# A state-space layer's carried products in halves of 64 rows: states kept in the scan's rows, two PSUM banks by the group's parity, and the third batch's W asked for later

## The chip, the cores and the metric

The kernel runs on one core of a Trainium2 chip. The metric is the device time of one execution in microseconds (us), the median of several. A profile of one execution gives the start and the length of every instruction on TensorE (PE, with its weight loads as PEld), VectorE (DVE), ScalarE (ACT), GpSimd (POOL) and the DMA queues, of which SyncE's (SP) carries nearly all loads.

## The reference

A trunk of two residual layers over 256 tokens of 2048 features: RMSNorm, a convolution module, RMSNorm, an MLP with squared ReLU; then the same with the state-space module in place of the convolution. Only the state-space module is touched:

```
u = h.reshape(bsz, L, 128, 16)                    # 128 groups of 16 channels
bu = einsum("blgc,gpc->blgp", u, bb)              # complex, 64 states a group
_, _, s_re, s_im = associative_scan(combine, (a, bu), axis=1)
y = einsum("blgp,gcp->blgc", s_re, c_re) - einsum("blgp,gcp->blgc", s_im, c_im)
y = gelu(y.reshape(bsz, L, 2048) + d_skip * h)
z = y @ w_glu;  val, gate = split(z, 2);  return val * sigmoid(gate)
```

All of it is in float32.

## The kernel before

The large products stream weights of 1 MB a step through SP; ACT rounds each half step to a high part (`hi`, L118), DVE forms the low part (`lo`, L125), and PE multiplies high by high, high by low and low by high (L222 to L224 in the layer at hand). A step has two halves of 12 such products. Three raw buffers are in turn, and a load is asked for when the low part of the step three before it is done.

The state-space layer sits between the first MLP and the second. The tokens are cut into 32 blocks of 8 (`CH`), and the scan runs over blocks. The groups are worked in four batches B of 32, each as 8 values g by 4 quarters q (the quarter picks 32 columns of the TensorE array and 32 partitions of PSUM). For a batch:

- `ssm_front` multiplies the inputs by table W (into the states), `ssm_turn` transposes, `ssm_scan` turns the complex scan into two real ones on DVE (`S`), and `ssm_forth` turns the result back (two products of 128x1024 into `t`).
- `ssm_states` forms the states `SS` from `t`. In the scan's layout the 128 rows are 64 states of two neighbouring groups: rows 0 to 63 belong to the group of even g, rows 64 to 127 to that of odd g. Before the change, `SS` has the real part in rows 0 to 63 and the imaginary part in rows 64 to 127, for each group; so each parity takes two DVE instructions over 64 rows, four in all, which move halves of the rows across.
- `ssm_local` multiplies the inputs by table M (what a block gives to itself); `ssm_carry` adds the states by table V (what is carried in) to the same PSUM banks `A`: 32 products, each over 128 rows, of 32 columns and 128 outputs. The two banks hold g 0 to 3 and 4 to 7. A float32 product shows in the trace as two matmul records with a weight load each. `ssm_carry` ends with GELU on ACT, and `ssm_out` transposes `y` into the features for the large product.

V is made during the first MLP as background work: 16 times `vstage` (three DVE products into the buffer `bv`, then one DMA on POOL's queue into `Vd` in DRAM), with `kstage` and `mstage` behind it, which make M.

`begin` writes the order for batches 0 and 1 by hand, before the first product with `w_glu`; batches 2 and 3, and what is left of batch 1, are put between half steps by the table `todo` (`carry(1)` in step 1, `carry(2)` in step 7, `carry(3)` in step 11). W, M, V, `xJ`, `S` and `yT` share the pool `blk` of six buffers. Which buffer a tile gets, and so what its load waits for, follows from the order in which the tiles are asked for. The loads of SP keep the order in which they are written.

Of the kernel before, what the change touches and what calls it, by code (L numbers as in the profile page):

```python
# [9 lines left out]
F32 = mybir.dt.float32  # L10
F32R = mybir.dt.float32r
I32 = mybir.dt.int32
AF = mybir.ActivationFunctionType
ALU = mybir.AluOpType
# [4 lines left out]
P = 128  # L19
# [8 lines left out]
G, ST, GC = 128, 64, 16  # L28
CH = 8
VW = PAD + T + 2  # L30
NQ = 4
# [5 lines left out]
class Trunk:  # L37
# [823 lines left out]
    def ssm_prep(self):  # L861
        nc, a, bg = self.nc, self.a, self.bg
# [2 lines left out]
        self.Wd = self.dram.tile([P, G, P], F32, name="Wd")  # L865
        self.Kd = self.dram.tile([G, GC, 15 * GC], F32, name="Kd")
        self.Md = self.dram.tile([P, G, P], F32, name="Md")
        self.Vd = self.dram.tile([P, G, P], F32, name="Vd")
        self.Bd = self.dram.tile([G, 2, ST, GC], F32, name="Bd")
        self.Rd = self.dram.tile([P, NQ, 1024], F32, name="Rd")  # L870
        self.xs = self.dram.tile([T, D], F32, name="xs")
        dma = nc.gpsimd.dma_start
# [221 lines left out]
        def vstage(k):  # L1094
            vs = s["bv"][:, 1, 0:1152].rearrange("p (g d c) -> p g d c", d=9, c=GC)
            g = slice(8 * k, 8 * k + 8)
            c = [s["c12"][:, i, g, :].unsqueeze(2).broadcast_to([P, 8, 8, GC]) for i in range(2)]
            p = [s[x][:, g, :].unsqueeze(3).broadcast_to([P, 8, 8, GC]) for x in ("pr", "pi")]
            t = self.t4([P, 8, 8, GC], name="vt")
            v = vs[:, :, 1:9, :]  # L1100
            self.tt(v, c[0], p[0], ALU.mult)
            self.tt(t, c[1], p[1], ALU.mult)
            self.tt(v, v, t, ALU.add)
            nc.scalar.activation(vs[:, :, 0, :], s["c12"][:, 0, g, :], AF.Copy)
            dma(out=self.Vd[:, g, :], in_=v.rearrange("p g d c -> p g (d c)"))

        def kstage(k):
            vs = s["bv"][:, 1, 0:1152].rearrange("p (g x) -> p g x", x=9 * GC)
# [17 lines left out]
        for k in range(16):  # L1126
            add(12, lambda k=k: vstage(k))
            add(4 if k < 4 else 3, lambda k=k: kstage(k))
            if k >= 4:
                for d in range(2 * (k % 4), 2 * (k % 4) + 2):  # L1130
                    add(0.5, lambda B=k // 4 - 1, d=d: mstage(B, d))
# [51 lines left out]
    def table(self, kind, B):  # L1183

        if kind == "R":
            t = self.t4([P, 2, 16, 32], name="R") if B != 2 else self.S[:, 1]
            self.fetch(t.rearrange("p i g j -> p (i g j)"), self.Rd[:, B])
        else:
            t = self.blk_tile([P, 32, P], name=kind + "t")
            src = {"W": self.Wd, "M": self.Md, "V": self.Vd}[kind]  # L1190
            for h in range(0, 32, 16):
                self.fetch(t[:, h:h + 16, :], src[:, 32 * B + h:32 * B + h + 16, :])
        self.tables[kind, B] = t

    def ssm_block(self, b):
# [79 lines left out]
    def ssm_scan(self, B, first=None):  # L1275

        nc = self.nc
        ps, R = self.X.pop(B), self.tables["R", B]
        S, t = self.S[:, 0], self.S[:, 2:4]
        m = self.t2([P, 16, 32], name="m")  # L1280
        with self.behind(self.pow_ins):
            nc.gpsimd.memset(m[:, :, 0], 0.0)
        with self.behind(self.xev0 if B == 0 else self.uev):
            nc.scalar.activation(m[:, :, 1:32], self.m8[:, 16 * B:16 * B + 16].unsqueeze(2).broadcast_to([P, 16, 31]), AF.Copy)
        ps = [p.rearrange("p g q j -> p q g j")[:, :, :, 0:31] for p in ps]
        re = lambda x: x.rearrange("p (q g) j -> p q g j", q=NQ)[:, :, :, 1:32]
        c, s = re(R[:, 0]), re(R[:, 1])
        t1, t2 = re(t[:, 0, 0]), re(t[:, 1, 0])
        self.tt(re(S[:, 0]), c, ps[0], ALU.mult)
        self.tt(t1, s, ps[1], ALU.mult)  # L1290
        self.tt(re(S[:, 1]), c, ps[1], ALU.mult)
        self.tt(t2, s, ps[0], ALU.mult)
        self.tt(re(S[:, 0]), re(S[:, 0]), t1, ALU.add)
        self.tt(re(S[:, 1]), re(S[:, 1]), t2, ALU.subtract)
        flat = lambda x: x.rearrange("p g j -> p (g j)")
        with self.behind(first) if first is not None else nullcontext():
            for i in range(2):
                ins = nc.vector.tensor_tensor_scan(out=flat(S[:, i]), data0=flat(m), data1=flat(S[:, i]), initial=0.0,
                                                   op0=ALU.mult, op1=ALU.add)
        return ins  # L1300
# [11 lines left out]
    def ssm_states(self, B):  # L1312
        nc = self.nc
        t = self.S[:, 2:4]
        SS = self.t4([P, 16, 2, 32], name="SS")
        for h in range(2):
            r = slice(64 * h, 64 * h + 64)
            self.tt(SS[0:64, :, h, :], t[r, 0, 0], t[r, 1, 1], ALU.subtract)
            self.scaled = nc.vector.tensor_tensor(out=SS[64:128, :, h, :], in0=t[r, 0, 1], in1=t[r, 1, 0], op=ALU.add)
        self.SS[B] = SS  # L1320

    def ssm_local(self, B, g0=0, g1=8):

        nc = self.nc
        M = self.tables["M", B]
        if B == 0:
            A = self.mv[B] = [self.bank([P, 4, CH, GC], name="mv"),
                              self.acc2()[:, 0].rearrange("p (g t c) -> p g t c", g=4, c=GC)]
        else:
            A = self.mv.setdefault(B, [])  # L1330
            A.extend(self.bank([P, 4, CH, GC], name="mv") for _ in range(g0 // 4, g1 // 4))
        U = self.xJ[:, B]
        for g in range(g0, g1):
            for q in range(NQ):
                self.mmm = nc.tensor.matmul(A[g // 4][32 * q:32 * q + 32, g % 4], lhsT=U[:, g, 32 * q:32 * q + 32],
                                 rhs=M[:, 8 * q + g, :], start=g % 4 == 0, stop=False, skip_group_check=True)

    def ssm_carry(self, B):

        nc = self.nc  # L1340
        SS = self.SS.pop(B)
        V = self.tables.pop(("V", B))
        A = self.mv.pop(B)
        for g in (0, 2, 4, 6, 1, 3, 5, 7):
            for q in range(NQ):
                self.vmm = nc.tensor.matmul(A[g // 4][32 * q:32 * q + 32, g % 4], lhsT=SS[:, 4 * q + g // 2, g % 2, :],
                                            rhs=V[:, 8 * q + g, :], start=False, stop=g % 4 == 3, skip_group_check=True)
        y = self.y = self.t4([P, CH, 8, GC], name="y")
        for g, t in (((0, slice(0, CH)), (4, slice(0, CH // 2)), (4, slice(CH // 2, CH))) if B == 0 else
                     ((0, slice(0, CH)), (4, slice(0, CH)))):  # L1350
            nc.scalar.activation(y[:, t, g:g + 4, :].rearrange("p t g c -> p g t c"), A[g // 4][:, :, t], AF.Gelu_apprx_tanh)

    def ssm_out(self, B):
        nc = self.nc
# [12 lines left out]
    def glu(self):  # L1367
# [4 lines left out]
        get = self.table  # L1372

        def begin():
            self.mv, self.SS = {}, {}
            self.ssm_start()
            self.ssm_scale(0)
            self.ssm_front(0)
            self.xev0 = self.xev
            self.ssm_turn(0)  # L1380
            self.ssm_scale(1)
            with self.behind(self.scaled):
                self.low_late()
            with self.behind(self.xtr):
                self.ssm_front(1)
            self.xJ_loads()
            get("M", 1)
            self.ssm_turn(1)
            xev = self.xev
            with self.behind(self.xtr):  # L1390
                self.ssm_local(0)
            get("V", 1)
            late = []
            with self.behind(xev):
                self.chunks[2](late)
                self.chunks[3](late)
            with self.behind(self.mmm):
                late[0]()
            with self.behind(self.ut):
                late[1]()  # L1400
            self.keep_warm(4, self.ut)
            get("W", 2)
            get("R", 2)
            self.ssm_forth(0, self.ssm_scan(0))
            self.ssm_states(0)
            self.ssm_carry(0)
            with self.behind(self.vmm):
                self.ssm_local(1, 0, 4)
            with self.behind(self.mmm):
                self.ssm_out(0)  # L1410
            with self.behind(self.yt):
                self.ssm_local(1, 4, 8)

            self.ssm_forth(1, self.ssm_scan(1, self.low))
            self.ssm_states(1)
            with self.behind(self.scaled), self.behind(xev):
                self.split(self.presplit, False)
            self.presplit += 1
            self.lo_gate = self.lo_ins
# [188 lines left out]
```

## Time and profile before

| | |
|---|---|
| median of 3 runs | 1987.88 us (1987.67 to 1988.95) |
| profiled execution | 1987.61 us, span 1985.8 us |
| granted TensorE clock | 0.999 of full speed |
| PE busy | 1966.9 us, 99% of the span |
| DVE, ACT, POOL busy | 71%, 48%, 14% |
| state-space layer, up to its last batch | from 1050 to 1160 us of the span |

PE is busy nearly always, so outside that stretch only what adds work to PE, or makes it wait, can change the time. Times in the trace count from the start of the span.

### The profile page before, as it was taken

What the parts mean: (1) busy time and instruction counts of PE and PEld (TensorE: products, weight loads), DVE (VectorE), ACT (ScalarE), POOL (GpSimd) and SP (SyncE); (2) the same over time, 40 slices, a digit from 0 to 9 for tenths busy, and PEclk for the clock granted to TensorE, in tenths of its full rate; (3) what the DMA queues carried; (4) which work ended last, traced back from release to release, by engine and by line L of the source; (5) the groups of instructions that cost most, each with busy time, mean ns of one, the idle gap of its engine ahead of it and who ended that gap; (6) DMA issues with size and microseconds to landing.
All of it is one profiled execution on the core that took longest, in us unless ns stands there. A gap on an engine that the chain in (4) does not pass through costs nothing.

```text
span 1985.8 us, 28885 instructions
## 1 busy us (share of the span) xinstructions
PE 1966.9 (99%) x11604; PEld 1687.0 (85%) x11604; DVE 1401.3 (71%) x1904; ACT 952.4 (48%) x1179; POOL 274.8 (14%) x252
## 2 busy tenths in 40 slices
PE   8999999999999999999999999999999999999998
PEld 8999788888888888888888788888888888888887
DVE  6899798888787777777558847565555565555655
ACT  6443655544444544444445445454444454444444
POOL 3998300000000221222010000000000000000000
PEclk9999999999999999999999999999999999999999
DMA  8767458667686877877898865665666656565653
GB/s 228 190 184 207 147 183 267 206 226 245 200 260 192 214 229 253 265 246 238 319 308 298 304 215 186 191 191 189 193 190 192 190 191 191 190 213 190 192 191 128
DMA packets 317030, 428.49 MB, mean 216 GB/s; under 512 B 9761, under 2 KB 211553, under 8 KB 313537
## 3 DMA queue, kind: packets, MB, share of 16 engines
q1 hardware_dynamic: 300976, 384.59, 61.6%
q0 software_dynamic: 12352, 37.49, 6.3%
q10 hardware_dynamic: 3568, 4.56, 0.8%
q8 instruction: 91, 1.49, 0.3%
q14 instruction: 43, 0.35, 0.1%
HBM read 400.08 MB, written 34.91 MB: 219 GB/s over the span
## 4 chain that ended last, share of the span: by engine, by line
PE 96%; DVE 2%; DMA 1%; issue 0%; SPq 0%; POOL 0%; ACT 0%; POOLq 0%; DVEq 0%; ACTq 0%
PE acc L199 24%; PE acc L222 15%; PE acc L223 15%; PE acc L224 15%; PE acc L202 12%; PE acc L213 3%; PE acc L212 3%; PE acc L211 3%; PE pk L484 1%; DMA Vt<-Vd 0%; SPq L92 0%; PE kp L1113 0%; PE xw L1254 0%; DMA raw<-in_conv_w_in_dram 0%; PE xt L254 0%
## 5 line engine op out<-in xcount | busy, mean ns | idle before, releaser
L118 ACT ACTIVATE hi<-raw 128x1024 fp32r<-128x1024 f32 x672 | 711.6, 1060 | 953.5 <-PE acc L224 510.2
L125 DVE TENSOR_TENSOR lo<-raw,hi 128x1024 fp32r<-128x1024 f32 x611 | 747.9, 1226 | 505.6 <-ACT hi L118 501.3
L199 PE MATMUL acc<-hT,hi 128*128 128x512 f32 x2048 | 514.4, 393 | 0.0
L199 PEld LDWEIGHTS acc<-hT,hi 128*128 128x128 f32 x2048 | 368.9, 189 | 68.0 <-issue 1.6
L222 PE MATMUL acc<-hi,rT 128*128 128x512 f32 x992 | 387.2, 391 | 0.0
L223 PE MATMUL acc<-lo,rT 128*128 128x512 f32 x992 | 386.4, 390 | 0.0
L224 PE MATMUL acc<-hi,rT 128*128 128x512 f32 x992 | 386.0, 389 | 0.0
L202 PEld LDWEIGHTS acc<-hT,lo 128*128 128x128 f32 x2048 | 279.6, 190 | 20.0
L202 PE MATMUL acc<-hT,lo 128*128 128x256 f32 x2048 | 286.3, 282 | 0.0
L222 PEld LDWEIGHTS acc<-hi,rT 128*128 128x128 f32 x992 | 186.3, 188 | 39.6 <-issue 1.6
L224 PEld LDWEIGHTS acc<-hi,rT 128*128 128x128 f32 x992 | 186.3, 188 | 39.1
L223 PEld LDWEIGHTS acc<-lo,rT 128*128 128x128 f32 x992 | 186.3, 188 | 38.0 <-issue 0.2
L125 POOL TENSOR_TENSOR lo<-raw,hi 128x1024 fp32r<-128x1024 f32 x60 | 143.1, 2402 | 31.3 <-ACT hi L118 24.8
L211 PE MATMUL acc<-hT,hi 128*128 128x256 f32 x512 | 146.1, 286 | 0.9 <-ACT hi L118 0.9
L212 PE MATMUL acc<-hT,hi 128*128 128x256 f32 x512 | 145.7, 286 | 0.3 <-DVE hT L259 0.3
L213 PE MATMUL acc<-hT,lo 128*128 128x256 f32 x512 | 145.5, 286 | 0.0
L829 DVE SCALAR_TENSOR_TENSOR cv<-vT,dw,cv 128x256 f32<-128x256 f32 x348 | 141.3, 486 | 2.2 <-ACT cv L527 1.7
L820 DVE TENSOR_TENSOR x<-x,acc 128x1024 f32<-128x1024 f32 (+1 forms) x72 | 83.6, 1161 | 27.6 <-PE acc L224 22.0
L211 PEld LDWEIGHTS acc<-hT,hi 128*128 128x128 f32 x512 | 98.9, 193 | 3.0 <-issue 1.6
L222 PE MATMUL acc<-hi,yT 128*128 128x512 f32 x256 | 101.1, 395 | 0.0
L212 PEld LDWEIGHTS acc<-hT,hi 128*128 128x128 f32 x512 | 98.8, 193 | 2.2 <-issue 1.6
L223 PE MATMUL acc<-lo,yT 128*128 128x512 f32 x256 | 99.9, 390 | 0.6 <-DVE lo L125 0.6
(285 smaller groups left out, 1722.9 us busy)
## 6 DMA issues: line engine op xcount, KB each, us to landing
raw<-in_mlp_w_up_dram SPq DMA_DIRECT2D x128, 1024.0 KB, 5.8
raw<-in_mlp_w_down_dram SPq DMA_DIRECT2D x128, 1024.0 KB, 5.2
raw<-in_ssm_w_glu_dram SPq DMA_DIRECT2D x32, 1024.0 KB, 5.5
raw<-in_conv_w_in_dram SPq DMA_DIRECT2D x60, 512.0 KB, 5.6
raw<-in_conv_w_out_dram SPq DMA_DIRECT2D x16, 1024.0 KB, 5.2
Vd<-bv POOLq DMA_DIRECT2D x16, 512.0 KB, 6.3
Md<-Kd POOLq DMA_DIRECT2D x32, 256.0 KB, 7.2
Wt<-Wd SPq DMA_DIRECT2D x8, 1024.0 KB, 10.1
```

The source lines that it names most:

```text
L118: self.nc.scalar.activation(hi, sl, AF.Copy)
L125: ins = eng.tensor_tensor(out=lo, in0=sl, in1=hi.bitcast(F32), op=ALU.subtract)
L199: mm(accs[m], lhsT=hi[:, kk, cs[m]], rhs=xT(k0 + kk), start=first and kk == 0, stop=False)
L202: mm(accs[m][:, 0:T], lhsT=lo[:, kk, cs[m]], rhs=xT(k0 + kk)[:, 0, :], start=False, stop=last and kk == 3)
L211: mm(accs[m], lhsT=hi[:, kk, c], rhs=x[:, 0, :], start=first and kk == 0, stop=False)
L212: mm(accs[m], lhsT=hi[:, kk, c], rhs=x[:, 1, :], start=False, stop=False)
L213: mm(accs[m], lhsT=lo[:, kk, c], rhs=x[:, 0, :], start=False, stop=last and kk == 3)
L222: mm(acc[:, b, :], lhsT=ak[:, 0, t], rhs=hi[:, kk, :], start=first and kk == 0, stop=False)
L223: mm(acc[:, b, :], lhsT=ak[:, 0, t], rhs=lo[:, kk, :], start=False, stop=False)
L224: self.mm_last = mm(acc[:, b, :], lhsT=ak[:, 1, t], rhs=hi[:, kk, :], start=False, stop=last and kk == 1)
L820: return self.nc.vector.tensor_tensor(out=out, in0=a, in1=b, op=op)
L829: return self.nc.vector.scalar_tensor_tensor(out=out, in0=a, scalar=s, in1=b, op0=op0, op1=op1)
```

## The change

Four things. `SS` keeps the scan's rows: part 0 is the real part, part 1 the imaginary, each one DVE instruction over 128 rows. The carried product of a group is therefore two products over 64 rows, one for each part, and V is stored in DRAM and on the chip in that form (four DMAs for a `vstage`, of half the rows and half the groups each; part 0 of a batch's V is the first of its two loads). The products of part 0 for all g come first, then those of part 1, taking the upper and the lower rows by turns, except in part 1 of batch 0, where bank 0 is finished first. The two banks hold the even and the odd g. And `begin` asks for W and R of batch 2 after `ssm_out(0)` and no longer before `ssm_scan(0)`.

```diff
-        self.Vd = self.dram.tile([P, G, P], F32, name="Vd")
+        self.Vd = self.dram.tile([P, NQ, 2, 16, P], F32, name="Vd")
...
-            dma(out=self.Vd[:, g, :], in_=v.rearrange("p g d c -> p g (d c)"))
+            for h in range(2):
+                for i in range(2):
+                    dma(out=self.Vd[64 * h:64 * h + 64, k // NQ, i, 4 * (k % NQ):4 * (k % NQ) + 4, :],
+                        in_=v[64 * i:64 * i + 64, h::2].rearrange("p g d c -> p g (d c)"))
...
-                self.fetch(t[:, h:h + 16, :], src[:, 32 * B + h:32 * B + h + 16, :])
+                src = self.Vd[:, B, h // 16] if kind == "V" else {"W": self.Wd, "M": self.Md}[kind][:, 32 * B + h:32 * B + h + 16, :]
+                self.fetch(t[:, h:h + 16, :], src)
...
-        SS = self.t4([P, 16, 2, 32], name="SS")
-        for h in range(2):
-            r = slice(64 * h, 64 * h + 64)
-            self.tt(SS[0:64, :, h, :], t[r, 0, 0], t[r, 1, 1], ALU.subtract)
-            self.scaled = nc.vector.tensor_tensor(out=SS[64:128, :, h, :], in0=t[r, 0, 1], in1=t[r, 1, 0], op=ALU.add)
+        SS = self.t4([P, 2, 16, 32], name="SS")
+        self.tt(SS[:, 0], t[:, 0, 0], t[:, 1, 1], ALU.subtract)
+        self.scaled = nc.vector.tensor_tensor(out=SS[:, 1], in0=t[:, 0, 1], in1=t[:, 1, 0], op=ALU.add)
...
+    def ssm_group(self, A, i):
+        g = 2 * (i % 4) + i // 4
+        return g, A[i // 4][:, i % 4]
...
-        for g in (0, 2, 4, 6, 1, 3, 5, 7):
-            for q in range(NQ):
-                self.vmm = nc.tensor.matmul(A[g // 4][32 * q:32 * q + 32, g % 4], lhsT=SS[:, 4 * q + g // 2, g % 2, :],
-                                            rhs=V[:, 8 * q + g, :], start=False, stop=g % 4 == 3, skip_group_check=True)
...
+        def products(part, i):
+            g, out = self.ssm_group(A, i)
+            r = slice(64 * (g % 2), 64 * (g % 2) + 64)
+            for q in range(NQ):
+                k = 4 * q + g // 2
+                self.vmm = nc.tensor.matmul(out[32 * q:32 * q + 32], lhsT=SS[r, part, k, :], rhs=V[r, 16 * part + k, :],
+                                            start=False, stop=part == 1 and i % 4 == 3, skip_group_check=True)
+        for i in (0, 4, 1, 5, 2, 6, 3, 7):
+            products(0, i)
+        for i in range(8) if B == 0 else (0, 4, 1, 5, 2, 6, 3, 7):
+            products(1, i)
...
-            get("W", 2)
-            get("R", 2)
             self.ssm_forth(0, self.ssm_scan(0))
             self.ssm_states(0)
             self.ssm_carry(0)
...
             with self.behind(self.mmm):
                 self.ssm_out(0)
+            get("W", 2)
+            get("R", 2)
```

On PE, the carried products of batch 0 (`Vt` is V, `mv` and `acc` are its two banks) stand between the filler products `warm` and the local products of batch 1 (`Mt` is M). Before:

```order
L189 MATMUL warm<-ident 128x128 x4
L1346 MATMUL mv<-Vt,SS 32x128 x8
L1346 MATMUL acc<-Vt,SS 32x128 x8
L1346 MATMUL mv<-Vt,SS 32x128 x8
L1346 MATMUL acc<-Vt,SS 32x128 x8
L1335 MATMUL mv<-Mt,xJ 32x128 x16
L1359 MATMUL yt<-ident,y 128x128 x8
```

With the change, at the same place:

```order
L1358 MATMUL mv<-Vt,SS 32x128 x4
L1358 MATMUL acc<-Vt,SS 32x128 x4
L1358 MATMUL mv<-Vt,SS 32x128 x4
L1358 MATMUL acc<-Vt,SS 32x128 x4
L1358 MATMUL mv<-Vt,SS 32x128 x4
L1358 MATMUL acc<-Vt,SS 32x128 x4
L1358 MATMUL mv<-Vt,SS 32x128 x4
L1358 MATMUL acc<-Vt,SS 32x128 x4
L1358 MATMUL mv<-Vt,SS 32x128 x16
L1358 MATMUL acc<-Vt,SS 32x128 x16
L1342 MATMUL mv<-Mt,xJ 32x128 x16
L1374 MATMUL yt<-ident,y 128x128 x8
```

The 32 products have become 64, of which the first 32 change banks, and so row halves, every four; what stands before and behind them is as it was.

On DVE, the states of batch 0 stand between `ssm_forth(0)` (the `S<-R,S` rows) and the scan of batch 1 (`S<-R,xtr`). Before:

```order
L820 TENSOR_TENSOR S<-R,S 128x1024 x2
L820 TENSOR_TENSOR SS<-S 64x16x32
L1319 TENSOR_TENSOR SS<-S 64x16x32
L820 TENSOR_TENSOR SS<-S 64x16x32
L1319 TENSOR_TENSOR SS<-S 64x16x32
L820 TENSOR_TENSOR S<-R,xtr 128x16x31 x4
```

With the change:

```order
L820 TENSOR_TENSOR S<-R,S 128x1024 x2
L820 TENSOR_TENSOR SS<-S 128x512
L1320 TENSOR_TENSOR SS<-S 128x512
L820 TENSOR_TENSOR S<-R,xtr 128x16x31 x4
L820 TENSOR_TENSOR S<-S 128x16x31 x2
```

Four instructions of 64 rows have become two of 128; the order around them is kept. SP's order is the same row for row.

## Rows read from the trace of the kernel before

**Rows 1.** The page: busy us of each engine, share of the span, instructions.
```profile
PE 1966.9 (99%) x11604; PEld 1687.0 (85%) x11604; DVE 1401.3 (71%) x1904; ACT 952.4 (48%) x1179; POOL 274.8 (14%) x252
```
**Rows 2.** Busy time by stretch: length, PE, PEld, DVE, ACT, POOL, clock, DMA share, GB/s.
```profile
640.00:940.00 300.00, 300.00 (x1736) 251.87 (x1735) 222.77 (x248) 140.81 (x180) 72.88 (x115) 1.00 0.79 239
```
**Rows 3.** What PE waited for, 1040 to 1160: us in total, times, longest.
```profile
PE mv L1346 <- DVE SS L1319: 1.9, 2, 1.5
...
PE mv L1346 <- DMA Vt<-Vd: 0.6, 1, 0.6
PE acc L223 <- DVE lo L125: 0.6, 1, 0.6
```
**Rows 4.** Timeline of batch 0: start, length, instruction, idle time before and its releaser.
```profile
1064.68 0.68 DVE L820 TENSOR_TENSOR SS<-S 64x512 f32<-64x512 f32 x1
1065.37 0.69 DVE L1319 TENSOR_TENSOR SS<-S 64x512 f32<-64x512 f32 x1
...
1066.11 0.65 PE L1346 MATMUL mv<-Vt,SS 128*32 128x128 f32 x16 [1.50 <-DVE SS L1319]
...
1067.55 0.65 PE L1346 MATMUL mv<-Vt,SS 128*32 128x128 f32 x16 [0.36 <-DVE SS L1319]
...
1068.26 0.60 ACT L1351 ACTIVATE y<-mv 128x512 f32<-128x512 f32 x1 [2.37 <-PE mv L1346]
...
1068.45 1.06 PE L1335 MATMUL mv<-Mt,xJ 128*32 128x128 f32 x32
1068.76 0.66 ACT L1351 ACTIVATE y<-acc 128x256 f32<-128x256 f32 x2
...
1069.44 1.09 PE L1359 MATMUL yt<-ident,y 128*128 128x128 f32 x8
```
**Rows 5.** Groups by form, 1060 to 1160: busy us, mean ns of one.
```profile
L820 DVE TENSOR_TENSOR xJ<-xJ,rJ 128x512 f32<-128x512 f32 x4 | 2.6, 684 | 0.0
...
L1351 ACT ACTIVATE y<-acc 128x256 f32<-128x256 f32 x2 | 0.7, 384 | 0.0
```
**Rows 6.** PE's timeline in windows from 1079.905 to 1080.040, and to 1080.066.
```profile
1079.91 0.32 PE L1346 MATMUL mv<-Vt,SS 128*32 128x128 f32 x4
...
1079.91 0.43 PE L1346 MATMUL mv<-Vt,SS 128*32 128x128 f32 x8
```
**Rows 7.** Records of line 1346, 1079 to 1083: ns of one (min/median/max), first and last start.
```profile
L1346 PE MATMUL mv<-Vt,SS x64: 272/273/297, 1079.9 to 1081.6; 128*32 128x128 f32 x64
```
**Rows 8.** PE's timeline, 1078.5 to 1085.8.
```profile
1079.91 1.96 PE L1346 MATMUL mv<-Vt,SS 128*32 128x128 f32 x64
...
1084.65 1.04 PE L1359 MATMUL yt<-ident,y 128*128 128x128 f32 x8
```
**Rows 9.** The chain that ended last, 1133 to 1155: start, us, what.
```profile
1138.87 1.24 DVE lo L125
...
1141.09 9.55 DMA Vt<-Vd
...
1150.69 1.94 PE mv L1346 x56
```
**Rows 10.** Busy time by stretch, columns as in Rows 2.
```profile
1060.00:1066.00 6.00, 4.62 (x84) 4.04 (x76) 5.82 (x6) 5.23 (x9) 0.13 (x1) 1.00 1.00 410
```
**Rows 11.** SP's own waits, 1060 to 1160.
```profile
SPq L92 <- PE acc L1335: 1.3, 1, 1.3
```
**Rows 12.** The load of `raw` asked for at 1063.1.
```profile
DMA to landing us min/median/max: 16.4/16.4/16.4
```
**Rows 13.** ACT's timeline, 1068 to 1110.
```profile
1080.02 1.06 ACT L118 ACTIVATE hi<-raw 128x1024 fp32r<-128x1024 f32 x1 [1.20 <-PE acc L224]
1081.49 1.09 ACT L1351 ACTIVATE y<-mv 128x512 f32<-128x512 f32 x2 [0.41 <-PE mv L1346]
```
**Rows 14.** POOL's issues by tile: ns of one (min/median/max), first and last start.
```profile
L1105 POOL DMA_DIRECT2D Vd<-bv x16: 892/932/941, 668.3 to 921.0; - x16
...
L1121 POOL DMA_DIRECT2D Kd<-ks x64: 507/507/547, 681.2 to 933.6; - x64
```

More of the change, by code (lines that the diff above doesn't have):

```diff
@@ L1189, in table @@
             t = self.blk_tile([P, 32, P], name=kind + "t")
-            src = {"W": self.Wd, "M": self.Md, "V": self.Vd}[kind]
             for h in range(0, 32, 16):
-                self.fetch(t[:, h:h + 16, :], src[:, 32 * B + h:32 * B + h + 16, :])
+                src = self.Vd[:, B, h // 16] if kind == "V" else {"W": self.Wd, "M": self.Md}[kind][:, 32 * B + h:32 * B + h + 16, :]
+                self.fetch(t[:, h:h + 16, :], src)
         self.tables[kind, B] = t
@@ L1292, in ssm_scan @@
         self.tt(t2, s, ps[0], ALU.mult)
+        flat = lambda x: x.rearrange("p g j -> p (g j)")
         self.tt(re(S[:, 0]), re(S[:, 0]), t1, ALU.add)
         self.tt(re(S[:, 1]), re(S[:, 1]), t2, ALU.subtract)
-        flat = lambda x: x.rearrange("p g j -> p (g j)")
         with self.behind(first) if first is not None else nullcontext():
@@ L1314, in ssm_states, with ssm_local @@
         t = self.S[:, 2:4]
-        SS = self.t4([P, 16, 2, 32], name="SS")
-        for h in range(2):
-            r = slice(64 * h, 64 * h + 64)
-            self.tt(SS[0:64, :, h, :], t[r, 0, 0], t[r, 1, 1], ALU.subtract)
-            self.scaled = nc.vector.tensor_tensor(out=SS[64:128, :, h, :], in0=t[r, 0, 1], in1=t[r, 1, 0], op=ALU.add)
+        SS = self.t4([P, 2, 16, 32], name="SS")
+        self.tt(SS[:, 0], t[:, 0, 0], t[:, 1, 1], ALU.subtract)
+        self.scaled = nc.vector.tensor_tensor(out=SS[:, 1], in0=t[:, 0, 1], in1=t[:, 1, 0], op=ALU.add)
         self.SS[B] = SS
-    def ssm_local(self, B, g0=0, g1=8):
+    def ssm_group(self, A, i):
+        g = 2 * (i % 4) + i // 4
+        return g, A[i // 4][:, i % 4]
+    def ssm_local(self, B, i0=0, i1=8):
         nc = self.nc
@@ L1330, in ssm_local @@
             A = self.mv.setdefault(B, [])
-            A.extend(self.bank([P, 4, CH, GC], name="mv") for _ in range(g0 // 4, g1 // 4))
+            A.extend(self.bank([P, 4, CH, GC], name="mv") for _ in range(len(A), (i1 + 3) // 4))
         U = self.xJ[:, B]
-        for g in range(g0, g1):
+        for i in range(i0, i1):
+            g, out = self.ssm_group(A, i)
             for q in range(NQ):
-                self.mmm = nc.tensor.matmul(A[g // 4][32 * q:32 * q + 32, g % 4], lhsT=U[:, g, 32 * q:32 * q + 32],
-                                 rhs=M[:, 8 * q + g, :], start=g % 4 == 0, stop=False, skip_group_check=True)
+                self.mmm = nc.tensor.matmul(out[32 * q:32 * q + 32], lhsT=U[:, g, 32 * q:32 * q + 32],
+                                 rhs=M[:, 8 * q + g, :], start=i % 4 == 0, stop=False, skip_group_check=True)
     def ssm_carry(self, B):
@@ L1343, in ssm_carry @@
         A = self.mv.pop(B)
-        for g in (0, 2, 4, 6, 1, 3, 5, 7):
+        y = self.y = self.t4([P, CH, 8, GC], name="y")
+        def products(part, i):
+            g, out = self.ssm_group(A, i)
+            r = slice(64 * (g % 2), 64 * (g % 2) + 64)
             for q in range(NQ):
-                self.vmm = nc.tensor.matmul(A[g // 4][32 * q:32 * q + 32, g % 4], lhsT=SS[:, 4 * q + g // 2, g % 2, :],
-                                            rhs=V[:, 8 * q + g, :], start=False, stop=g % 4 == 3, skip_group_check=True)
[L1348 to L1351, printed above, removed]
+                k = 4 * q + g // 2
[5 more added lines that the diff above has]
+            products(1, i)
+        for h in range(2):
+            for t in (slice(0, CH // 2), slice(CH // 2, CH)) if B == 0 and h else (slice(0, CH),):
+                nc.scalar.activation(y[:, t, h::2, :].rearrange("p t g c -> p g t c"), A[h][:, :, t], AF.Gelu_apprx_tanh)
     def ssm_out(self, B):
```

## Prediction

> **What bounds the kernel now.** The page's first part comes first: PE is busy for 1966.9 of 1985.8 us [rows 1], so the question is where PE waits, and what adds work to it. The busy time by stretch answers for the first MLP, where V is made: PE is busy for 300.00 of 300 us there [rows 2], so nothing in that stretch can be won, and something is lost only if a high or low part comes late. The list of PE's waits over 1040 to 1160 us holds the rest: 1.9 us in two waits for `SS`, 0.6 us for a load of V, 0.6 us for a low part [rows 3]. The timeline places the first two waits in batch 0: PE idles 1.50 us before the carried products, and 0.36 us in the middle of them [rows 4]. The reader is to see a chain there (states, products, GELU, transposes) in which each link is waited for; in the later batches the same products stand in a stream in which PE has no idle time but the two waits of 0.6 us. The forecast is therefore a sum of three terms: what batch 0 gains, what the load of V gains, and what 64 products of 64 rows cost PE in batches 1 to 3 against 32 of 128.
>
> **States.** Four DVE instructions of 64x512 take 0.68 or 0.69 us each, and start 0.69 us apart [rows 4]. The two new ones are 128x512; the nearest row of that shape, also with both inputs and the output on the chip, took 684 ns [rows 5]. A row's length goes with its elements per partition and not with the rows, so I take 0.68 us. Before, PE began at 1066.11, just after the second instruction had ended at 1065.37 + 0.69 = 1066.06. Now part 0 needs the first alone: 1064.68 + 0.68 + 0.05 = 1065.41, which is 0.70 us earlier. Part 1's states are ready by 1066.05, before part 0's products are through, so the wait of 0.36 us goes too.
>
> **The products.** Before: the first four records of a carry start within 0.32 - 0.30 = 0.02 us (the longest record, a first one, is 297 ns [rows 7]), none follows in the first 0.13 us, and the eighth closes at 0.43 [rows 6]. So four go side by side, one for each quarter of the columns, and a round of four takes 0.11 us: 64 records are 16 rounds, 1.75 us, of the 1.96 us that the whole carry shows with its first and last latency [rows 8]. The issue of four inside 0.02 us says that sixteen rounds are what the array needs, and that issuing is not the limit. Now there are 128 records. If the two row halves work side by side as the four column quarters do, eight go in a round and the 16 rounds stay 16: cost 0. If the halves do not overlap, there are 32 rounds: 1.75 us more a batch. No record before uses fewer than 128 rows in two halves, so both ends stay in the range; I take the first, since the column quarters behave exactly so, and put 0 to 0.1 us a batch on it for filling eight places where four were filled.
>
> [...]
>
> **Batch 0.** Part 0 runs from 1065.41 in eight rounds to 1066.29. Part 1 takes first the four even g, all in the upper rows, then the four odd ones. If PE issues far enough ahead these overlap too (0.88 us), if not they take 1.75 us: the local products of batch 1 then start at 1067.2 or 1068.0, against 1068.45 [rows 4]. They take 0.99 us, up to the transposes. The transposes also need the first GELU (0.60 us) and half of the second (384 ns) [rows 4, 5]. In the early case both banks end near 1067.4, the GELUs start 0.50 us apart as before, and the transposes may start at 1068.4; in the late case bank 0 has its GELU done meanwhile and PE is the last: 1069.0. Before it was 1069.44. The gain is 1.0 or 0.4 us; I take 0.7. Behind the transposes the chain (ACT, local products, first product with `w_glu`) moves as a whole, and DVE, which is needed for the low part of `yT`, is 1.4 us further ahead than PE.
>
> **The load of V in batch 3.** The chain shows the low part at 1138.87, behind the four `SS` instructions, then SP's loads, then `Vt`, 9.55 us, then the carry at 1150.69 [rows 9]. With two `SS` instructions fewer the low part and the load come 1.4 us earlier, which is more than the wait of 0.6 us [rows 3]. Besides, part 0 needs only the first of the two loads. Gain 0.6 us. The third wait, 0.6 us for a low part [rows 3], comes behind the scan and the turning back of batch 2 on DVE, with no `SS` instruction among them, and stays.
>
> **Edits costed at nothing.** (a) V's storing: 48 more DMAs on POOL's queue. One of `Vd` takes 0.93 us of POOL, the smaller ones of `Kd` 0.51 us [rows 14]; four of the latter against one of the former are 1.1 us more, 16 times, 18 us in all. They hide in POOL's idle 227 of 300 us [rows 2]. Behind them queue the `Kd` and `Md` DMAs, which batch 0's load of M comes long after, and DVE's next write to `bv`; DVE has 77 of the 300 us idle. Without that cover PE would lose what DVE loses. (b) The order of the background work on DVE and ACT shifts by an instruction here and there; hidden by the same slack. (c) W and R of batch 2: SP keeps its order, but in the built program W takes the buffer that batch 0's V leaves, at the end of the carry (about 1068), and no longer the one that batch 0's M leaves, for which SP waited 1.3 us [rows 11]. Queued behind it are R and the fourth `raw`, and ACT waits for that. The DMA engines are saturated from 1060 to 1066 (share 1.00 at 410 GB/s [rows 10]) with batch 1's M and V in front, so an earlier request for W mostly waited in their line: I expect `raw` to land 0 to 1 us later than before.
>
> **Sum.** -0.7 (batch 0) - 0.6 (V) + 0.2 (three fillings of 0 to 0.1 us) = -1.1 us. The profiled execution took 1987.61 us, the median is 1987.88; forecast 1986.8 us for the median, own range 1985.6 to 1987.5. A measurement of this kernel tells a change from none at about 0.2%, 4 us.
>
> **Rivals.**
> 1. *The row halves do not overlap* (or an issue floor on the average): three batches by 1.75 us are +5.2; in batch 0 the 32 rounds end at 1065.41 + 3.5 = 1068.9, half a microsecond later than before, +0.5; the load of V still gives 0.6. Sum +5.1, 1993.0 us: slower by 0.26%. [...] It decides from 1.6 us of extra PE time a batch on. Chance 0.14.
> 2. *The halves overlap in part*: say the two records of a float32 product keep their order within a group of four, so that a half has to wait for its own first record before the other may start. Then a group of four products takes one round of 0.11 us and a start of 0.03 us where the half is its own, 64 products 16 x 0.14 = 2.2 us: +0.45 a batch, +1.3 for three; batch 0 gains 0.3, V 0.6: +0.4, 1988.3 us. No measurable change. Chance 0.2.
> 3. *The fourth `raw` comes late and ACT stands in front of it.* ACT's queue has its high part at 1080.02, right before the GELU of batch 1 at 1081.49 [rows 13], which PE's transposes need at 1084.65 [rows 8]. The load landed at 1063.1 + 16.4 = 1079.5 [rows 12]. The transposes would be held if it landed after 1084.65 - 0.7 - 1.09 - 1.06 - 0.1 = 1081.7, 2.2 us later than before, and then by as much as it is later. I expect at most 1 us. Up to 1990 us. Chance 0.04.
> 4. *Faster by over 4 us*: the waits listed come to 3.1 us [rows 3], so something outside the argument would have to move. Chance 0.02.
>
> **How the numbers follow.** My forecast has 0.60. It, rival 2 (0.2) and half of rival 3 (0.02) stay within 0.2%: same 0.82. Slower 0.15: rival 1 and what of rival 3 comes on top of rival 2's price. Faster 0.03: rival 4 and what I have not seen. Eight times in ten the time should lie between 1985.2 (both gains at their upper end, 1.0 + 0.7, and the spread of the runs) and 1990.0, which takes in rival 2 and most of rival 3 and leaves rival 1 out.
>
> **What would show it.** Right: in carries 1 to 3, 128 records in 1.9 to 2.1 us; PE at `SS` products at 1065.4, with one wait of about 0.8 us; transposes of batch 0 at 1068.4 to 1069.0; no wait for `Vt` at 1150; the high part of the fourth `raw` still before 1081.7. Wrong: a carry of 3.5 us, eight records that start in two groups of four 0.11 us apart, or PE waiting for `y`.

## The result, and the profile after

| | before | after |
|---|---|---|
| median | 1987.62 us (1987.12 to 1989.20, 22 runs) | 1990.28 us (1988.52 to 1991.68, 22 runs) |
| profiled execution, span | 1987.61 us, 1985.8 us | 1991.12 us, 1989.3 us |
| granted TensorE clock | 0.999 | 0.998 |

The ratio is 1.0012, with a 95% interval of 1.0007 to 1.0018: 2.7 us slower, where 1.1 us faster was forecast. The median lies 0.3 us above 1985.2 to 1990.0, the range that was to hold eight times in ten, and further above the narrower own range of 1985.6 to 1987.5. The runs after the change also spread over 3.2 us, those before over 2.1.

The list of PE's waits comes first. Of after, 1060 to 1160 us (total, times, longest):

```profile
PE mv L1342 <- issue: 2.5, 1, 2.5
PE mv L1358 <- DVE SS L820: 0.8, 1, 0.8
PE acc L223 <- DVE lo L125: 0.6, 1, 0.6
```

Against [rows 3], one wait for `SS` is gone and the other is shorter, and the wait for `Vt` is gone, as forecast. The first line is new: PE stands for 2.5 us in the local products of batch 1, and "issue" says that it waits for nothing in the program that the profile shows. PE's timeline of after places it (start, length, instruction, records, idle time before):

```profile
1064.09 1.15 PE L189 MATMUL warm<-ident 128*128 128x128 f32 x8
1066.05 0.31 PE L1358 MATMUL mv<-Vt,SS 64*32 64x128 f32 x4 [0.81 <-DVE SS L820]
1066.08 0.31 PE L1358 MATMUL acc<-Vt,SS 64*32 64x128 f32 x4
1066.18 0.29 PE L1358 MATMUL mv<-Vt,SS 64*32 64x128 f32 x4
...
1068.43 0.64 PE L1342 MATMUL mv<-Mt,xJ 128*32 128x128 f32 x14
1071.55 0.88 PE L1342 MATMUL mv<-Mt,xJ 128*32 128x128 f32 x18 [2.48 <-issue]
1072.36 1.97 PE L1374 MATMUL yt<-ident,y 128*128 128x128 f32 x8
1074.26 1.70 PE L1342 MATMUL mv<-Mt,xJ 128*32 128x128 f32 x32
1075.89 0.50 PE L222 MATMUL acc<-hi,yT 128*128 128x512 f32 x1
```

The same place before (`warm` at 1063.46 and the first product with `w_glu` at 1071.47 are not in the rows shown earlier):

```profile
1063.46 1.16 PE L189 MATMUL warm<-ident 128*128 128x128 f32 x8
...
1070.46 1.08 PE L1335 MATMUL mv<-Mt,xJ 128*32 128x128 f32 x32
1071.47 0.50 PE L222 MATMUL acc<-hi,yT 128*128 128x512 f32 x1
```

Counted from `warm`, so that the 0.63 us by which this execution is late already ahead of the layer drop out (0.59 of it stands at 229 us, before any of the changed lines has run): the local products start at 4.34 us instead of 4.99 [rows 4], a gain of 0.65. The transposes start at 8.27 instead of 5.98, so 2.94 us are lost in the 16 local products, which stop after 14 of their 32 records. Then the eight transposes last 1.90 us to the next start instead of 1.02, and the next local products 1.63 instead of 1.01. The busy time by stretch says why (length, PE, PEld, DVE, ACT, POOL, clock, DMA share, GB/s):

```profile
1066.00:1069.00 3.00, 2.95 (x142) 2.55 (x143) 3.00 (x6) 1.45 (x5) 0.00 (x0) 1.00 1.00 421
1069.00:1071.60 2.60, 0.12 (x7) 0.05 (x7) 1.09 (x2) 0.22 (x1) 0.00 (x0) 1.00 0.87 306
1071.60:1076.00 4.40, 4.40 (x59) 3.51 (x59) 1.69 (x3) 1.19 (x2) 0.00 (x0) 0.61 1.01 414
1076.00:1080.00 4.00, 4.00 (x18) 3.27 (x19) 3.97 (x4) 0.56 (x1) 0.00 (x0) 1.00 0.84 293
```

After PE has stood, its granted clock is 0.61 on average from 1071.6 to 1076 (0.50 of full speed from 1072.2 to 1075.5), and then 1.00 again. Standing and slow clock together cost 2.94 + 0.88 + 0.62 = 4.44 us. The later carries do what was forecast; carry 1 and 3 of after, and carry 3 of before:

```profile
1084.32 2.03 PE L1358 MATMUL mv<-Vt,SS 64*32 64x128 f32 x128
...
1154.08 2.03 PE L1358 MATMUL mv<-Vt,SS 64*32 64x128 f32 x128
```
```profile
1149.42 0.63 PE L1346 MATMUL mv<-Vt,SS 128*32 128x128 f32 x8
1150.69 1.94 PE L1346 MATMUL mv<-Vt,SS 128*32 128x128 f32 x56 [0.64 <-DMA Vt<-Vd]
```

128 records take 2.03 us, against 1.96 for 64 [rows 8]. Carry 3 took 1152.63 - 1149.42 = 3.21 us before and takes 2.03 now. Carries 1 and 2 take 2.03 us after, and 1.96 and 1.98 before. The account is -0.65 (batch 0) + 4.44 - 1.18 (carry 3) + 0.12 (carries 1 and 2) = +2.73 us, against 2.66 between the medians.

### The profile page after: what moved, and what is told of

It reads as the page before. It is cut to its first block, busy times and chain, and to the rows that moved or that the text cites. A ratio compares the mean times of both kernels' runs of the same rounds, so it can differ in the third digit from the quotient of the medians.

```text
span 1989.3 us, 29457 instructions
## 1 busy us (share of the span) xinstructions
PE 1969.3 (99%) x11860; PEld 1688.6 (85%) x11860; DVE 1394.0 (70%) x1896; ACT 952.2 (48%) x1179; POOL 299.1 (15%) x300
## 3 DMA queue, kind: packets, MB, share of 16 engines
q8 instruction: 93, 1.52, 0.3%
## 4 chain that ended last, share of the span: by engine, by line
PE 97%; DVE 1%; issue 1%; POOL 0%; DMA 0%; ACT 0%; SPq 0%; POOLq 0%; DVEq 0%; ACTq 0%
PE acc L199 24%; PE acc L222 16%; PE acc L223 15%; PE acc L224 15%; PE acc L202 12%; PE acc L213 3%; PE acc L211 3%; PE acc L212 3%; PE pk L484 1%; PE xt L254 1%; PE kp L1116 0%; PE mv L1342 0%; PE xw L1257 0%; PE mv L1358 0%; PE stat L539 0%
## 5 line engine op out<-in xcount | busy, mean ns | idle before, releaser
L118 ACT ACTIVATE hi<-raw 128x1024 fp32r<-128x1024 f32 x672 | 711.5, 1060 | 952.3 <-PE acc L224 505.8
L199 PEld LDWEIGHTS acc<-hT,hi 128*128 128x128 f32 x2048 | 368.8, 189 | 67.9 <-issue 1.6
L202 PEld LDWEIGHTS acc<-hT,lo 128*128 128x128 f32 x2048 | 279.6, 190 | 20.0
L211 PEld LDWEIGHTS acc<-hT,hi 128*128 128x128 f32 x512 | 98.9, 193 | 3.0 <-issue 1.6
L213 PEld LDWEIGHTS acc<-hT,lo 128*128 128x128 f32 x512 | 98.5, 193 | 2.0 <-POOL lo L125 1.1
```

The source lines that it names most:

```text
L118: self.nc.scalar.activation(hi, sl, AF.Copy)
L199: mm(accs[m], lhsT=hi[:, kk, cs[m]], rhs=xT(k0 + kk), start=first and kk == 0, stop=False)
L202: mm(accs[m][:, 0:T], lhsT=lo[:, kk, cs[m]], rhs=xT(k0 + kk)[:, 0, :], start=False, stop=last and kk == 3)
L211: mm(accs[m], lhsT=hi[:, kk, c], rhs=x[:, 0, :], start=first and kk == 0, stop=False)
L213: mm(accs[m], lhsT=lo[:, kk, c], rhs=x[:, 0, :], start=False, stop=last and kk == 3)
```

## The theory, and the experiments

A float32 product is two weight loads and two matmuls for PE (carry 1 of after, 64 products, shows 128 records of each). Among the DMA queues of the page, one of kind "instruction" has 93 packets and 1.52 MB, 16 KB a packet. Before it had 91, for 2 x 11604 PE instructions [rows 1]; now there are 2 x 11860. 512 more for two packets is 256 a packet; from these counts I take its packets to be PE's instructions. Part 3 of the page after, and the packets between 1069.1 and 1069.4 us:

```profile
q8 instruction: 93, 1.52, 0.3%
```
```profile
q8 instruction: 1, 0.02, 21.5%
```

From 1059.9 to 1069.1 us there is none. So PE stands from 1069.06 while a packet that begins to move behind 1069.1 is on its way. T1: the carry of batch 0 now takes 256 PE instructions in 2.4 us, and PE runs out of them. T2: PE waits for a load or a bank that the trace doesn't name. T3: the requests at 1068.56 to 1070.69, which the change moved there, delay it.

Times of before here are those of the same chip; each ratio is against them.

**W and R back.** The part that T3 blames, undone:

```diff
+            get("W", 2)
+            get("R", 2)
             self.ssm_forth(0, self.ssm_scan(0))
...
-            get("W", 2)
-            get("R", 2)
             with self.behind(self.yt):
```

> One part undone: the third batch's W and R are requested before the scan of batch 0 again, as in the kernel before; states, products and banks stay as changed. In the changed kernel PE stands still for 2.48 us in the middle of local(1) (1069.06 to 1071.55), with nothing in the program that it waits for, and its granted clock is about 0.55 from 1072 to 1076. T1 (PE runs out of instructions: its program comes over the instruction queue in packets of 16 KB, 93 now and 91 before, which is one for 256 PE instructions; the carry of batch 0 now takes 256 of them in 2.4 us, and the packet that PE needs next was moved only at 1069.20 to 1070.23): the standstill stays at the same instructions, 1 to 3 us long, and the time stays at 1988.5 to 1991.7. T3 (the requests at 1068.56 to 1070.69, which this change moved, delay PE): the standstill is gone and the time is 1985.5 to 1986.8. T2 (PE waits for a load or a bank that the trace does not name): the standstill stays, and it stays in the next two runs as well.

1991.27 us (before 1987.73; 1.0017, 1.0009 to 1.0026). PE's timeline of this run:

```profile
1068.20 0.64 PE L1342 MATMUL mv<-Mt,xJ 128*32 128x128 f32 x14
1072.43 1.44 PE L1342 MATMUL mv<-Mt,xJ 128*32 128x128 f32 x18 [3.60 <-issue]
```

The standstill is at the very same record, and longer. T3 falls.

**More PE instructions far ahead.** At 229 us PE fills a wait with nine products of the identity. Some are replaced, so that only the count of PE instructions ahead of the layer changes; the order of all else on the engines is that of the changed kernel (with 256, splits of weights change places on DVE and ACT in the stretch behind it, and one on DVE in the layer):

```diff
-        self.keep_warm(9, self.bc)
+        self.keep_warm(2, self.bc); self.keep_warm(24, self.bc, small=64)
```

`small=64` multiplies 32 columns of the identity by 64 columns. 24 x 4 - 7 x 4 = 68 instructions more; 71 small products make 256, one packet; the control has 68 in the kernel before.

> The changed kernel with 68 more PE instructions far ahead of the layer (at 229 us, where PE fills a wait of 2.2 us with small products: 7 of 9 of them are replaced by 24 of 32x64). Everything behind is the same on every engine, but the points at which one packet of 256 instructions ends and the next begins lie 68 instructions earlier in the program, so that PE reaches one ahead of its wait for the states of batch 0 and the next in the middle of the carry. T1: no standstill in local(1), no fall of the clock there, and 1985.5 to 1986.8: the changed kernel's 1990.28 less 2.5 us of standstill and less 1.5 to 2 us of slow clock. T2 and T3: the standstill stays, 1988.5 to 1991.7.

1986.64 us (before 1987.73; 0.9994, 0.9985 to 1.0003). PE's timeline of this run, local products of batch 1 and carry 1:

```profile
1067.54 1.08 PE L1342 MATMUL mv<-Mt,xJ 128*32 128x128 f32 x32
1068.55 1.09 PE L1374 MATMUL yt<-ident,y 128*128 128x128 f32 x8
...
1079.01 2.01 PE L1358 MATMUL mv<-Vt,SS 64*32 64x128 f32 x126
1081.49 0.38 PE L1358 MATMUL mv<-Vt,SS 64*32 64x128 f32 x2 [0.47 <-issue]
1081.80 0.50 PE L222 MATMUL acc<-hi,yT 128*128 128x512 f32 x1
```

The standstill in the local products is gone, 3.6 us of median with it, and T2 falls too. A small one stands in carry 1 instead, two records before its end: from its start to the next product 2.79 us pass, 0.83 more than in the carry of after (1084.32 to 1086.28). The clock stayed at 1.00 there (1081 to 1086), so the expectation of a later run is wrong in naming a slower clock.

> The same edit with 256 more PE instructions (71 small products of 32x1 in place of 7), one whole packet, so that the ends of packets lie where they lay in the changed kernel. T1: the standstill is back at the same place of local(1), 1 to 3 us long, with the fall of the clock behind it; the time is 3 to 5 us above that of the run with 68, plus what the longer filling costs at 229 us (up to 2 us): 1989 to 1993. T2 and T3: the standstill was never away. If it is gone here as well, the number of instructions ahead does not decide it by packets of 256, and T1 falls.

1996.22 us (before 1987.73; 1.0037, 1.0025 to 1.0050). PE's timeline of this run:

```profile
1072.30 0.64 PE L1342 MATMUL mv<-Mt,xJ 128*32 128x128 f32 x14
1075.30 1.44 PE L1342 MATMUL mv<-Mt,xJ 128*32 128x128 f32 x18 [2.37 <-issue]
```

A whole packet more, and PE stops again after 14 of 32 records: the count of instructions ahead, in packets, decides the place. The total is 3 us over the expected range, because the longer filling cost more at 229 us than the 2 us allowed for: the next product starts at 236.04 instead of 232.40 in the changed kernel, though this execution was 0.62 us ahead until then, and the clock is 0.72 from 229 to 236 and 0.89 from 236 to 250:

```profile
229.00:236.00 7.00, 7.00 (x148) 6.83 (x148) 7.00 (x15) 5.61 (x12) 0.10 (x1) 0.72 0.43 152
```

> The control: the kernel before with the same 68 PE instructions at 229 us. T1: its carry of batch 0 has 128 PE instructions in place of 256, which leaves a packet longer to come, so there is no standstill of PE at either position: 1987.3 to 1988.0, as the kernel before. If the added products by themselves make a kernel faster (a higher clock behind them, say), it shows here: then 1986.5 or less, and the run with 68 tells less.

1987.72 us (before 1987.73; 0.9999, 0.9990 to 1.0008): the added products are worth nothing by themselves.

**Another 28, and half a packet.** 31 and 39 small products of 32x32, in the changed kernel.

> The changed kernel with 96 more PE instructions at 229 us (31 small products of 32x32 in place of 7 of the 9 that fill the wait). With 68 more the standstill in local(1) was gone, but 0.47 us of another stood in the carry of batch 1 at 1081.03, with a slower clock behind it (0.90 us in all). T1, with the ends of packets counted through the program: 28 instructions further neither the local products nor the carries have two ends of packets closer than the 5.8 us or so that a packet took to come in the stalled runs, but for 0.5 us at most at 1075, so the 0.90 us come back: 1985.3 to 1986.3, faster than both kernels. If the place of the ends does not matter and 68 was good by chance, the standstill is back: 1988.5 to 1991.7.

1985.84 us (1985.62 to 1986.86 in 11 runs; before 1987.43, 1986.94 to 1989.45 in 33; 0.9991, 0.9982 to 1.0000). That is within the 0.2% of the forecast, but the ranges do not overlap: the slowest of these runs is faster than the fastest of before. By the medians this version is 1.6 us faster than the kernel before, and over 4 us faster than the changed one. PE's waits from 1060 to 1160 us hold no "issue" any more:

```profile
PE mv L1358 <- DVE SS L820: 0.8, 1, 0.8
PE acc L223 <- DVE lo L125: 0.6, 1, 0.6
PE xtr L1274 <- ACT X L1260: 0.3, 1, 0.3
```

> The changed kernel with 128 more PE instructions, half a packet. T1, counted the same way: an end of a packet falls on the first products of the carry of batch 2 (about 1122 us), and the next on its last ones, 256 instructions or some 2.3 us later; so PE stands still there, between 0.5 and 3.5 us, with a slower clock behind it, and not in local(1) of batch 1: 1986.5 to 1990.5. Rival: a standstill is bound to the stretch with full DMA engines (1060 to 1078 us); then there is none at 1122 us, where the engines have spare time, and the time is that of the run with 96.

1986.87 us (before 1987.43; 0.9997, 0.9988 to 1.0005). PE's timeline of this run, around carry 2:

```profile
1122.29 2.03 PE L1358 MATMUL mv<-Vt,SS 64*32 64x128 f32 x128
1124.25 0.50 PE L222 MATMUL acc<-hi,yT 128*128 128x512 f32 x1
1124.60 0.39 PE L223 MATMUL acc<-lo,yT 128*128 128x512 f32 x1
1125.75 0.50 PE L224 MATMUL acc<-hi,yT 128*128 128x512 f32 x1 [0.77 <-issue]
```

The standstill has moved to carry 2, as counted, two products behind it. The rival is not settled by this run: the DMA share was 1.01 from 1122.3 to 1125 as well.

**The parts.** W and R later alone, in the kernel before, and W and R early again in the run with 96:

> One part alone: the kernel before with the third batch's W and R requested behind the second batch's first local products, and nothing else. Both theories: 1987.3 to 1988.1, no change that can be measured, for the packet that PE needs at 1073 comes in time either way; against it: ACT's queue has one gelu later behind a split of weights, which could cost up to 1 us at 1080.

> The run with 96 more instructions, with the third batch's W and R requested before the scan of batch 0 again. If the later request is worth something by itself, it shows here against the run with 96. T1: PE is not stalled in either, so the same within 0.5 us, 1985.3 to 1986.8; but the first run had a longer standstill with the early request (3.60 against 2.48 us), so a packet comes later while W and R load, and up to 1 us of standstill may appear here.

1987.36 us (before 1987.43; 0.9999, 0.9990 to 1.0008) and 1986.05 us (before 1987.43; 0.9993, 0.9984 to 1.0002; 0.2 us above the run with 96). The moved requests are worth nothing that can be measured, alone or with the rest.

Batch 0's products and states as in the kernel before, with V of batch 0 in its old form, and all else as changed:

```diff
+        if B == 0:
+            for i in range(8):
+                g, out = self.ssm_group(A, i)
+                for q in range(NQ):
+                    self.vmm = nc.tensor.matmul(out[32 * q:32 * q + 32], lhsT=SS[:, 4 * q + g // 2, g % 2, :],
+                                                rhs=V[:, 8 * q + g, :], start=False, stop=i % 4 == 3, skip_group_check=True)
```

> One part undone: the states and the carried products of batch 0 are made as in the kernel before (states in the products' rows, 64 products over 128 rows), those of batches 1 to 3 as changed, W and R later as changed; with the 68 instructions ahead that keep ends of packets away from the three changed carries. T1: batch 0 has 128 carry instructions and cannot run dry, but it loses its gain of 0.6 to 0.7 us; the load of V for batch 3 still costs nothing (1.2 us of gain): 1986.2 to 1987.0, between the kernel before and the run with 96 more instructions. Rival: all of the gain is in batch 0; then 1987.3 to 1987.9.

> The same without instructions ahead. Against the changed kernel 128 PE instructions are gone in the carry of batch 0, so the ends of packets behind it lie as in the run with 128 more. T1: no standstill at 1069 us, and one of 0.5 to 1 us behind the carry of batch 2 at about 1125 us: 1986.8 to 1988.0. Rival (the standstill comes from the new layout of V, from the banks by parity or from the later requests, all of which this kernel has): it stays at 1069 us, and 1988.5 or more.

With 68 more: 1987.06 us (before 1987.64; 0.9997, 0.9988 to 1.0006), between what was expected (up to 1987.0) and the rival (1987.3 and more). This median doesn't settle how much of the gain belongs to batch 3; its list of waits has none for `Vt`. Without: 1987.84 us (before 1987.64; 1.0000, 0.9992 to 1.0009). In both traces the `issue` wait at 1069 us is gone, though the banks and the requests are the changed ones, and so is V's layout in batches 1 to 3. The second's list of waits begins:

```profile
PE mv L1373 <- DVE SS L1325: 1.5, 1, 1.5
PE acc L223 <- DVE lo L125: 0.6, 1, 0.6
PE acc L222 <- issue: 0.5, 1, 0.5
```

The last of these is at 1126.12 us, behind carry 2, as with 128 more: 128 instructions fewer or more is the same place in a packet. So it is the carry's 256 instructions that empty the supply.

The kernel before bears this out. Up to this carry its PE instructions are those of the changed kernel, so a packet is begun at the same place, some 14 records into the carry, at 1066.47 us. The next packet begins to move at 1069.81, which is later than the 1069.20 of the changed kernel. Of before, 1069.75 to 1070:

```profile
q8 instruction: 1, 0.02, 25.3%
```

But the 256 instructions in hand keep PE busy to 1072.76, and it doesn't stop; in the changed kernel they were through at 1069.06.

**The supply by itself.** In the kernel before, 300 small products of 32x1 stand in place of 7 at 229 us, once in turn on four column groups, once on one with 64 columns:

```diff
+                if small:
+                    ps = self.wps[32 * (j % 4):32 * (j % 4) + 32, 0:small]
```

> The supply of instructions measured by itself: the kernel before with 300 small products (1200 PE instructions, of 32 columns by 1) in place of 7 at 229 us, in turn on four column groups of the array. The local products of this kernel, in four column groups as well, run 128 instructions in about 1.9 us, 15 ns each. T1: a packet of 256 takes over 5 us to be replaced, so the stretch shows standstills of PE about 256 instructions apart, 1 to 2 us each, at least three of them, and takes 20 to 28 us. Rivals (PE waits for something else in the changed kernel): no standstill, and some 18 us. The whole kernel gets slower by the length of the stretch, 15 to 30 us.

2004.51 us, one run (before 1987.64). PE's timeline of this run:

```profile
229.51 2.23 PE L191 MATMUL warm<-ident 128*128 128x128 f32 x186
234.79 1.89 PE L191 MATMUL warm<-ident 128*32 128x1 f32 x128 [3.05 <-issue]
238.25 1.89 PE L191 MATMUL warm<-ident 128*32 128x1 f32 x128 [1.57 <-issue]
241.97 1.89 PE L191 MATMUL warm<-ident 128*32 128x1 f32 x128 [1.84 <-issue]
245.98 0.65 PE L191 MATMUL warm<-ident 128*32 128x1 f32 x34 [2.12 <-issue]
```

Here T1 is to be seen bare. Between two standstills lie exactly 128 matmul records, with their loads 256 instructions. PE is through with them in 1.89 us, and the next are there 3.46, 3.72 and 4.01 us after the last. The stretch takes 17.1 us and not the 20 to 28 expected, since a packet came faster than the over 5 us that were taken from batch 0. By stretch:

```profile
229.50:247.00 17.50, 8.92 (x606) 8.42 (x605) 15.79 (x38) 12.98 (x25) 3.03 (x4) 0.65 0.27 88
247.00:252.00 5.00, 5.00 (x20) 3.44 (x19) 4.64 (x31) 0.49 (x2) 0.00 (x0) 0.52 0.36 98
```

The DMA engines are busy for 0.27 of the time, so a standstill does not need full ones. The granted clock is 0.65 in the first stretch and 0.52 in the second; but with 256 more it fell at this place too (0.72 above), where PE worked through 32x1 products and did not stand, so this fall is not shown to come from the standstills.

> The control for it: the same 1200 instructions in one column group, with 64 columns moving, which took about 30 ns each in the run with 68. 256 of them last some 7.7 us, longer than the 5.8 us that a packet took in the stalled runs. T1: no standstill over 0.3 us, about 36 us for the stretch. If standstills show here as well, packets take longer than 7.7 us.

2018.87 us, one run. The 1200 instructions take 34 us, 256 of them 7.3, and PE does not stand: it is busy for all of 34.50 us at full clock.

```profile
229.50:264.00 34.50, 34.50 (x607) 34.24 (x606) 31.66 (x137) 13.50 (x27) 3.06 (x5) 1.00 0.19 60
```

**One count over all traces.** The lists of PE's waits have ten waits on "issue" in seven of the traces and none in the others. Count all PE rows of the trace ahead of each: weight loads, matmuls, and the few semaphore and drain rows that the views leave out. There are 13505 in the changed kernel and with W and R back, 13761 with 256 more, 14017 with 68, 15041 with 128, 14785 in the second run with batch 0 as before, and 4289, 4545, 4801 and 5057 with four column groups. Divided by 256, every one leaves 193. Ahead of each of the ten, a packet of the instruction queue begins to move 2.2 to 2.9 us before PE goes on. And of the blocks of 256 rows that lie between such places, each of the ten that PE ran through in 2.6 us or less was followed by a stop, and none that took 4.2 us or more. A wait for a load or a bank (T2) would not keep to this count.

## Why the prediction was wrong, step by step

- **The products: right for the array, wrong for what feeds it.** The row halves work side by side: eight records start from 1066.05 on and the next at 1066.18, and carries 1 and 2 grew by 0.07 and 0.05 us, within the 0 to 0.1 forecast. Rivals 1 and 2 are out, and no run shows the issue floor that rival 1 names beside the halves: the 128 records of carry 1 start some 15 ns apart on average (1.96 us up to the next product). So is rival 3 out: PE's list has no wait for a GELU. The step that failed stands right there: "that issuing is not the limit". It was read off four records, and the doubled count was costed by the array's rounds alone. Four instructions a product make 256 in a carry, a whole packet, spent in 2.4 us where before it was half of one, and no rival named the supply. What the runs showed in place of the step: the array keeps up with 128 records in 2.03 us, but the next packet isn't there when PE is through with the one in hand, and PE stood for 2.48 us.
- **Batch 0: right up to the local products, then wrong.** 0.65 us were gained against 0.7 forecast. But "the chain moves as a whole" behind the transposes did not hold: the standstill fell between, and took the gain with 4.44 us: 2.94 in the local products where PE stopped, 1.50 by the slow clock in the transposes and local products behind them.
- **The load of V: mechanism right, size 0.6 against 1.18.** The wait [rows 3] counts from the modelled end of the records before, 0.63 us after they began. But only 8 had started, and the other 56 took all of their 1.94 us behind it. The loss is read by the whole carry, 3.21 us against 2.03.
- **Edits at nothing: right.** The moved requests changed nothing that can be measured, alone or in the run with 96. With the early requests the standstill is longer in the one profile (3.60 against 2.48 us), but the intervals of the two kernels overlap. POOL's extra DMAs (busy 299.1 us against 274.8 [rows 1]) cost nothing that shows.
- **The sum with the term left out** is the account above. Where the ends of packets are out of the way, -0.65 - 1.18 + 0.12 = -1.7 us is what remains, and the run with 96 more gained 1.6.

The wider spread of the runs may go with it, though that is argued and not shown: the standstill lasted 2.48 us in the changed kernel's profile, and 3.60 and 2.37 us in those of the two runs that stop at the same record.

## What to carry to other kernels

Before work is cut into more and smaller products, count PE's instructions, four for a float32 product, and mark where 256 of them pass in less time than a packet needs here (3.0 to 6.4 us from the start of the one before it): there PE can run dry (here it did at 2.6 us and less, and not at 4.2 us and more), and an idle time put down to "issue" right after a dense stretch was the sign here. Whether it does hung on where the ends of packets fall (68 or 96 instructions more ahead took the stop in batch 0 away, 256 more left it), so an edit far ahead can bring it or take it away; test it with a few instructions more ahead before the edit at hand is blamed. And read a short wait by how long the whole group took, not by the idle time alone.

## What the runs showed of the hardware that was not expected

Between the stops with four column groups, a packet of 256 PE instructions is replaced 3.5 to 4.0 us after it was begun, with the DMA engines at 0.27. In the layer, by counting 256 instructions back from each stop, it took 5.3 us in the changed kernel (from 1066.2 to 1071.55), 6.4 with W and R early, 3.0 at carry 1 and 3.4 at carry 2. What makes it late in batch 0 is open; the DMA engines' share was full there (1.00 from 1066 to 1069 us) and at carry 2 (1.01) alike. The kernel before was near the edge: if PE has a packet 2.2 to 2.9 us after it begins to move, an estimate from the ten stops, the one of 1069.81 was there at 1072.0 to 1072.7, and PE needed it at 1072.76. Around and behind the end of the stops of 2.37, 2.48 and 3.60 us in batch 0 the granted clock was 0.66 (1075 to 1080), 0.61 (1071.6 to 1076) and 0.60 (1072 to 1079); behind those of 0.47 to 0.77 us, and behind the wait of 1.50 us for `SS` in the kernel before, it stayed at 1.00. And 128 records of 64x32 tiles start within 2.0 us, some 15 ns apart on average (1.96 us from the first of carry 1 to the next product); in batch 0 eight start from 1066.05 us on and the ninth at 1066.18.
